# Stick-breaking attention: the scans of a pair of query rows queued behind the last low part of the pair ahead

## Chip, cores and metric

The kernel runs on one core of one Trainium2 chip. The metric is the device time of one execution in microseconds (us), as the median of the runs shown.

## The reference

A hybrid decoder layer over 1024 tokens of width 1024: a SwiGLU feed-forward block, a token mixer, a second feed-forward block, each on an RMS-normalised input, and a final normalisation. The mixer has 8 stick-breaking attention heads of width 64 and 4 gated recurrent heads (HGRN2) of width 128. The change lies in the attention heads:

```
z = einsum('bhqd,bhkd->bhqk', q_blk, k) * scale
causal = key_pos < q_pos
log_beta = log_sigmoid(z)
log_rest = where(causal, log_sigmoid(-z), 0)
tail = cumsum(log_rest, axis=3, reverse=True) - log_rest
w = where(causal, exp(log_beta + tail), 0)
o = einsum('bhqk,bhkd->bhqd', w, v)
```

So a weight is sigmoid(z) times the product of sigmoid(-z) over all later keys before the query. Everything is float32.

## The kernel before, in words

The tokens are stored in reverse order, so that "all keys between" is a running product from the left. Every float32 matmul is made of three in a rounded type: a number is split in a high part H (a rounding copy on ScalarE, L122) and a low part L (the source minus H, L123, on VectorE unless another engine is named). `split` does both.

The mixer works through four head pairs p; each pair p is two attention heads (a = 0, 1) and one recurrent head. `attend` (L761) runs the attention of a head pair: over two halves of the tokens (hf), two heads (a), and two pairs of query rows (qp) of two blocks of 128 rows each (j = 2 qp and 2 qp + 1). That makes 8 pairs of rows for each p and 32 in all.

For each block of rows, `stick` (L728) computes the scores of up to 512 keys at a time (TensorE, L743 to L746, in one of two banks ps_z), takes sigmoid(-z) into `rest` and sigmoid(z) into `beta` (ScalarE, L749 and L750), runs the running product over `rest` (VectorE's scan, L751; 128 to 512 columns) and multiplies it into `beta` (VectorE, L753; L755 multiplies the first column by the carry of the scan before). A block in the first half of the keys has two such steps chained by the carry, one in the second half has one, so a pair of rows has 4 or 2 scans, 96 in all.

When both blocks of a pair are done, the weights are transposed in units of two key blocks (m = qp to 3): TensorE transposes 3 or 4 blocks into one of two banks tp (L798, L799), ScalarE writes the high part wH, VectorE the low part wL (both L123's `split`, called in L804), each of two buffers, and TensorE multiplies them with the values into `po` (L769), one turn later than the transposes. A pair has 4, 3, 2 or 1 such units, 80 low parts in all. Here the first unit of a pair has 384 columns and the others 512. After two pairs, `po` is copied and added into the output `o_sb` (L811 on ScalarE, L813 on VectorE).

Between two calls of `stick` the generator yields, and the recurrent head takes a step of its own (`scan_half`, L840: small products on VectorE at L850, L869 and L895, predicated copies at L880, matmuls at L863 and L887). Behind each attention stretch come the projections of the next head pair (`project`, L663, three matmuls a step through L126 to L128; their outputs are read by L687, L697, L826, L836 and L837).

The order on each engine is not the order of the program. A scheduler lays all instructions out beforehand by its own timeline: on each engine it takes what it holds to be ready, earlier lines of the program first. A block `with tc.issue_after(ins):` adds an edge of order alone from each instruction inside that runs on the engine of `ins`: it is queued behind `ins` on that engine, without a semaphore. The kernel uses it already, among others for the products with the values (`in_turn`, L180, behind the last transpose).

Of the kernel before, what the change touches and what calls it, by code (L numbers as in the profile page):

```python
# [8 lines left out]
F32 = mybir.dt.float32  # L9
# [4 lines left out]
ALU = mybir.AluOpType  # L14
# [13 lines left out]
def hybrid_layer(ctx: ExitStack, tc, xT, gains, wg1, wu1, wd1, w_in, lbl, w_out, wg2, wu2, wd2, outT):  # L28
# [8 lines left out]
    nc = tc.nc  # L37
# [82 lines left out]

    def split(dH, dL, src, eng=None):
        nc.scalar.copy(dH, src)  # L122
        (eng or nc.vector).tensor_tensor(dL, src, dH.bitcast(F32), op=ALU.subtract)  # L123

    def mm3(ps, w, a, first, last):
        nc.tensor.matmul(ps, lhsT=w[0], rhs=a[0], start=first, stop=False)  # L126
# [3 lines left out]
    class Weights:  # L130
# [5 lines left out]
        def load(self, src, eng=None):  # L136
            r = self.raw.tile([P, self.width], F32, tag="raw", name="raw")
            nc.sync.dma_start(r, src)
            H = self.unit.tile([P, self.width], F32R, tag="uH", name="uH")
            L = self.unit.tile([P, self.width], F32R, tag="uL", name="uL")  # L140
            split(H, L, r, eng)
            return H, L
# [34 lines left out]
    def pe(ins):  # L177
        last_pe[:] = [ins.ins]

    def in_turn():  # L180

        return tc.issue_after(last_pe[0]) if last_pe else nullcontext()
# [54 lines left out]
    def norm_h(hf, g0, cols=slice(0, HALF), eng=None):  # L237
        for r in row_rstd(hf, cols):
            yield
        for c in range(NKC):  # L240
            if cols.start == 0:
                h[c, hf] = [hp.tile([P, HALF], F32R, tag=n, name=n) for n in ("hH", "hL")]
            t = xp.tile([P, HALF], F32, tag="x", name="hf")[:, cols]
            nc.vector.scalar_tensor_tensor(t, x[c, hf][:, cols], gn[:, g0 + c:g0 + c + 1], r,
                                           op0=ALU.mult, op1=ALU.mult)
            split(h[c, hf][0][:, cols], h[c, hf][1][:, cols], t, eng(c) if eng else None)
            yield
# [6 lines left out]
    def ffn(wg, wu, wd, order, prepare, on_x, on_half, pieces, g0, shared):  # L254
        one, two = order
        with ExitStack() as st:
# [22 lines left out]
            def entry(src, pool=None, eng=None):  # L279

                p, tH, tL = (hx, "bH", "bL") if pool is hx else (unit, "uH", "uL")
                H = p.tile([P, HALF], F32R, tag=tH, name=tH)
                L = p.tile([P, HALF], F32R, tag=tL, name=tL)
                split(H, L, src, eng)
                return H, L
# [368 lines left out]
    with ExitStack() as mix:  # L654
# [52 lines left out]
        def project_vi(p, vs, vg):  # L707

            ws = [W.load(w_in[VI + 4 * p + i], nc.gpsimd) for i in range(4)]
            for b2 in range(4):  # L710
# [14 lines left out]
                vg += [t[:, 0], t[:, 1]]  # L725
                yield

        def stick(q, k, a, j):  # L728

            out = {}  # L730
            S = q[j // 4][a]
            qc = slice((j % 4) * P, (j % 4 + 1) * P)
            carry = None
            for kh in range(j // 4, 2):
                b0 = max(j, 4 * kh)
                n = (4 * kh + 4 - b0) * P
                nw = max(n, 256)
                z0 = nw - n
                kc = slice(HALF - nw, HALF)
                H, L = k[kh][0][a], k[kh][1][a]  # L740
                z = ps_z.tile([P, HALF], F32, tag="z", name="z")
                diag = carry is None
                nc.tensor.matmul(z[:, :nw], lhsT=S[:, qc], rhs=H[:, kc], start=True, stop=False)  # L743
                pe(nc.tensor.matmul(z[:, :nw], lhsT=S[:, qc], rhs=L[:, kc], start=False, stop=not diag))
                if diag:
                    nc.tensor.matmul(z[:, z0:z0 + P], lhsT=ident_b, rhs=negm, start=False, stop=True)  # L746
                rest = mp.tile([P, HALF], F32, tag="rest", name="rest", bufs=3)
                beta = mp.tile([P, HALF], F32, tag="beta", name="beta", bufs=5)
                nc.scalar.activation(rest[:, :n], z[:, z0:nw], AF.Sigmoid, scale=-1.0)  # L749
                nc.scalar.activation(beta[:, :n], z[:, z0:nw], AF.Sigmoid)  # L750
                nc.vector.tensor_tensor_scan(rest[:, :n], rest[:, :n], rest[:, :n],  # L751
                                             1.0 if diag else carry, ALU.mult, ALU.bypass)
                nc.vector.tensor_tensor(beta[:, 1:n], beta[:, 1:n], rest[:, :n - 1], op=ALU.mult)  # L753
                if not diag:
                    nc.vector.tensor_tensor(beta[:, 0:1], beta[:, 0:1], carry, op=ALU.mult)  # L755
                carry = rest[:, n - 1:n]
                for b in range(b0, 4 * kh + 4):
                    out[b] = beta[:, (b - b0) * P:(b - b0 + 1) * P]
            return out

        def attend(p, q, k, vs, hfs=(0, 1)):  # L761

            later = []

            def products(po, vs, a, qp, m, H, L):
                for i in range(2):
                    b = 2 * m + i
                    for w in (H, L):
                        nc.tensor.matmul(po[:, (qp % 2) * 256:(qp % 2) * 256 + 256],  # L769
                                         lhsT=vs[b // 2][:, b % 2, a], rhs=w[:, 256 * i:256 * i + 256],  # L770
                                         start=m == qp and i == 0 and w is H,
                                         stop=m == 3 and i == 1 and w is L)

            def turn(*args):
                while later:
                    products(*later.pop())
                if args:
                    later.append(args)

            for hf in hfs:  # L780
                ot = xp.tile([P, HALF], F32, tag="x", name="o_sb")
                ov = ot.rearrange("p (q j t) -> p q j t", q=2, j=2)
                for a in range(2):
                    rows = slice(64 * a, 64 * a + 64)
                    po = ps_po.tile([P, HALF], F32, tag="po", name="po", bufs=1)
                    for qp in (2 * hf, 2 * hf + 1):
                        w0 = stick(q, k, a, 2 * qp)
                        yield
                        w1 = stick(q, k, a, 2 * qp + 1)
                        yield  # L790
                        for m in range(qp, 4):
                            tp = ps_tp.tile([P, HALF], F32, tag="tp", name="tp")
                            H = mp.tile([P, HALF], F32R, tag="wH", name="wH")
                            L = mp.tile([P, HALF], F32R, tag="wL", name="wL")
                            for i in range(2):
                                b = 2 * m + i
                                if b > 2 * qp:
                                    pe(nc.tensor.transpose(tp[:, 256 * i:256 * i + P], w1[b], ident))  # L798
                                pe(nc.tensor.transpose(tp[:, 256 * i + P:256 * i + 256], w0[b], ident))  # L799
                            lo = P if m == qp else 0  # L800
                            if m == qp:
                                nc.gpsimd.memset(H[:, :P].bitcast(F32), 0.0)
                                nc.gpsimd.memset(L[:, :P].bitcast(F32), 0.0)
                            split(H[:, lo:], L[:, lo:], tp[:, lo:])  # L804
                            with in_turn():
                                turn(po, vs, a, qp, m, H, L)
                    turn()
                    pv = po.rearrange("p (q j t) -> p q j t", q=2, j=2)
                    low = slice(64 - 64 * a, 128 - 64 * a)
                    for j in range(2):  # L810
                        nc.scalar.copy(ov[rows, :, j], pv[rows, :, 1 - j])  # L811
                    for j in range(2):
                        nc.vector.tensor_tensor(ov[rows, :, j], ov[rows, :, j], pv[low, :, 1 - j], op=ALU.add)  # L813
                o[2 * p, hf] = ot
# [217 lines left out]
        for n, _ in enumerate(attend(3, q, k, vs, (1, 0))):  # L1032
            next(scan)
            for _ in range({0: 1, 2: 1, 4: 1, 6: 1, 8: 1, 9: 1, 10: 1, 11: 1, 12: 1, 13: 1, 14: 1, 15: 1}.get(n, 0)):
                next(outs, None)
            if n == 8:
                state = out_half(3, 1, K[1], Q[1], *scans[1], vg, state)
            if n == 10:
                head_norms([(o[7, 1], True, 31, gate[1]), (o[6, 1], False, 27, None)])
            if n == 10 + 1:  # L1040
                mix_in(7, 1)
                mix_in(6, 1)
# [124 lines left out]
```

## Time and profile before

| what | value |
|---|---|
| median of 3 runs | 1984.62 us (1983.78 to 1987.51) |
| the profiled execution, its own time | 1987.7 us |
| its span | 1986.0 us |
| TensorE busy (matmul) | 1924.8 us, 97% |
| VectorE busy | 1343.5 us, 68% |
| ScalarE busy | 804.4 us, 41% |
| GpSimd busy | 948.0 us, 48% |
| scans, L751 | 96, 98.4 us in all |
| products, L753 | 96, 61.2 us in all |
| low parts of the weights, wL at L123 | 80, 49.4 us in all |

The span runs from the first to the last instruction of the profile. In the rows PE is TensorE, PEld its weight loads, DVE is VectorE, ACT is ScalarE, POOL is GpSimd. Busy time is the time in which an engine shows at least one instruction. Ends of matmuls are modelled and may overlap the next. A row of a timeline has the start from the span's beginning, the duration, engine, line, operation, what it writes and reads with shapes, and in brackets the idle time of its engine just before it and what ended it; rows in order of time may merge neighbours of one kind (x2).

### The profile page before, as it was taken

Reading aid. Unit: us, or ns where it says so; the run is one execution under the profiler, and the core shown is the slowest. Engines: PE = TensorE matmul, PEld = TensorE weight load, DVE = VectorE, ACT = ScalarE, POOL = GpSimd, SP = SyncE. Lnnn points to the kernel's source line nnn. Section 1 sums busy time; section 2 is a strip of 40 time slices with the busy share of each in tenths; the row PEclk is TensorE's granted clock in tenths of the full one; section 3 lists DMA queues with packets and bytes.
Section 4 is the critical chain, followed back from the end, with each engine's and each line's share of the span. In section 5 each row is a group of like instructions: output and inputs, shape, how many; then the busy total and the mean of one; then the engine's idle time right before and its main releaser. Section 6 shows DMA issues by size and latency. Waiting matters only on the chain.

```text
span 1986.0 us, 29345 instructions
## 1 busy us (share of the span) xinstructions
PE 1924.8 (97%) x10938; PEld 1589.0 (80%) x10938; DVE 1343.5 (68%) x1898; ACT 804.4 (41%) x1489; POOL 948.0 (48%) x815
## 2 busy tenths in 40 slices
PE   9899999999999999999999999999999999999997
PEld 7678888887888787887987977878778878888886
DVE  7966676667456736838648469669776666674476
ACT  6333323324444444535435445444333223344443
POOL 5245566557757432322233252001465565577585
PEclk9999999999999999999999999999999999999999
DMA  5134445346765421110111121211253454457544
GB/s 205 50 117 149 148 157 173 133 148 203 229 200 188 140 64 38 39 43 23 33 54 28 38 80 40 84 64 65 90 173 126 152 186 149 148 182 227 191 165 154
DMA packets 107823, 242.07 MB, mean 122 GB/s; under 512 B 10400, under 2 KB 12448, under 8 KB 107680
## 3 DMA queue, kind: packets, MB, share of 16 engines
q1 hardware_dynamic: 107392, 240.16, 36.7%
q8 instruction: 86, 1.41, 0.3%
q14 instruction: 57, 0.47, 0.1%
q10 hardware_dynamic: 288, 0.02, 0.0%
HBM read 169.89 MB, written 66.06 MB: 119 GB/s over the span
## 4 chain that ended last, share of the span: by engine, by line
PE 78%; DVE 9%; POOL 6%; issue 3%; DMA 2%; ACT 2%; SPq 0%; POOLq 0%; DVEq 0%; ACTq 0%
PE acc L126 17%; PE acc L128 17%; PE acc L127 17%; PE pj L126 3%; PE pj L128 3%; PE pj L127 3%; DMA raw<-in_wd_dram 2%; PE po L769 2%; PE pv L126 2%; PE pv L128 2%; PE pv L127 2%; PE wo L126 1%; DVE rest L751 1%; PE wo L127 1%; PE wo L128 1%
## 5 line engine op out<-in xcount | busy, mean ns | idle before, releaser
L122 ACT CAST uH<-raw 128x512 fp32r<-128x512 f32 x360 | 215.0, 619 | 499.8 <-POOL raw L354 187.9
L123 DVE TENSOR_TENSOR uL<-raw,uH 128x512 fp32r<-128x512 f32 x308 | 287.1, 949 | 167.9 <-ACT uH L122 167.7
L126 PE MATMUL acc<-hH,uH 128*128 128x512 f32 x704 | 280.4, 399 | 11.6 <-ACT uH L122 6.4
L127 PE MATMUL acc<-hL,uH 128*128 128x512 f32 x704 | 276.5, 393 | 0.3 <-DVE hL L228 0.2
L128 PE MATMUL acc<-hH,uL 128*128 128x512 f32 x704 | 271.1, 395 | 0.7 <-DVE uL L123 0.7
L123 DVE TENSOR_TENSOR bL<-raw,bH 128x512 fp32r<-128x512 f32 x140 | 168.7, 1211 | 136.0 <-ACT bH L122 117.8
L123 POOL TENSOR_TENSOR bL<-raw,bH 128x512 fp32r<-128x512 f32 x140 | 203.1, 1459 | 106.6 <-ACT bH L122 103.9
L122 ACT CAST bH<-raw 128x512 fp32r<-128x512 f32 x280 | 160.5, 618 | 188.5 <-PE acc L127 79.1
L373 DVE TENSOR_TENSOR c<-c,acc 128x512 f32<-128x512 f32 x280 | 186.9, 679 | 64.4 <-PE acc L128 62.1
L127 PE MATMUL acc<-bL,bH 128*128 128x512 f32 (+1 forms) x576 | 220.8, 383 | 0.9 <-DVE bL L123 0.9
L126 PE MATMUL acc<-bH 128*128 128x512 f32 (+1 forms) x576 | 221.2, 384 | 0.0
L128 PE MATMUL acc<-bH,bL 128*128 128x512 f32 (+1 forms) x576 | 219.1, 383 | 0.0
L126 PE MATMUL acc<-bH,uH 128*128 128x512 f32 x480 | 186.7, 389 | 0.6 <-ACT uH L122 0.6
L127 PE MATMUL acc<-bL,uH 128*128 128x512 f32 x480 | 186.7, 389 | 0.0
L128 PE MATMUL acc<-bH,uL 128*128 128x512 f32 x480 | 186.7, 389 | 0.0
L126 PEld LDWEIGHTS acc<-hH,uH 128*128 128x128 f32 x704 | 133.7, 190 | 51.9 <-ACT uH L122 19.0
L128 PEld LDWEIGHTS acc<-hH,uL 128*128 128x128 f32 x704 | 132.9, 189 | 35.3 <-DVE uL L123 8.3
L127 PEld LDWEIGHTS acc<-hL,uH 128*128 128x128 f32 x704 | 133.7, 190 | 28.1 <-DVE hL L228 1.5
L352 POOL TENSOR_TENSOR raw<-raw 128x512 f32<-128x512 f32 x40 | 60.0, 1501 | 194.7 <-DVE uL L123 194.7
L442 POOL TENSOR_TENSOR raw<-raw 128x512 f32<-128x512 f32 x20 | 27.0, 1352 | 263.8 <-DMA raw<-in_wd_dram 244.0
L123 POOL TENSOR_TENSOR uL<-raw,uH 128x512 fp32r<-128x512 f32 x52 | 70.1, 1354 | 155.6 <-ACT uH L122 152.3
L127 PEld LDWEIGHTS acc<-bL,bH 128*128 128x128 f32 x576 | 108.3, 188 | 22.2 <-DVE bL L123 1.3
(237 smaller groups left out, 4321.3 us busy)
## 6 DMA issues: line engine op xcount, KB each, us to landing
raw<-in_wd_dram SPq DMA_DIRECT2D x74, 512.0 KB, 4.3
a<-c SPq DMA_DIRECT2D x140, 256.0 KB, 3.2
raw<-a SPq DMA_DIRECT2D x70, 512.0 KB, 4.7
raw<-in_wg_dram SPq DMA_DIRECT2D x40, 512.0 KB, 4.8
raw<-in_wu_dram SPq DMA_DIRECT2D x40, 512.0 KB, 4.6
w<-raw SPq DMA_DIRECT2D x40, 512.0 KB, 2.8
raw<-w SPq DMA_DIRECT2D x40, 512.0 KB, 3.8
raw<-in_w_in_dram SPq DMA_DIRECT2D x56, 256.0 KB, 2.7
```

Source lines behind the costliest of these rows:

```text
L122: nc.scalar.copy(dH, src)
L123: (eng or nc.vector).tensor_tensor(dL, src, dH.bitcast(F32), op=ALU.subtract)
L126: nc.tensor.matmul(ps, lhsT=w[0], rhs=a[0], start=first, stop=False)
L127: nc.tensor.matmul(ps, lhsT=w[0], rhs=a[1], start=False, stop=False)
L128: pe(nc.tensor.matmul(ps, lhsT=w[1], rhs=a[0], start=False, stop=last))
L352: tt(a22, a21, a22, op=ALU.add)
L373: nc.vector.tensor_tensor(out, a, ps, op=ALU.add)
L442: tt(a22, a21, a22, op=ALU.add)
L751: nc.vector.tensor_tensor_scan(rest[:, :n], rest[:, :n], rest[:, :n], 1.0 if diag else carry, ALU.mult, ALU.bypass)
L769: nc.tensor.matmul(po[:, (qp % 2) * 256:(qp % 2) * 256 + 256], lhsT=vs[b // 2][:, b % 2, a], rhs=w[:, 256 * i:256 * i + 256], start=m == q ...
```

## The change

`split` returns its subtraction. A list holds the last low part of the pair of rows traced last (that of m = 3), and the scans of every later `stick` are queued behind it on VectorE. It carries over from one head, half and head pair to the next; only the two blocks of the very first pair have no such edge. Nothing else of the source changes.

```diff
     def split(dH, dL, src, eng=None):
         nc.scalar.copy(dH, src)
-        (eng or nc.vector).tensor_tensor(dL, src, dH.bitcast(F32), op=ALU.subtract)
+        return (eng or nc.vector).tensor_tensor(dL, src, dH.bitcast(F32), op=ALU.subtract)
...
+        last_low = []
+
         def stick(q, k, a, j):
...
-                nc.vector.tensor_tensor_scan(rest[:, :n], rest[:, :n], rest[:, :n],
-                                             1.0 if diag else carry, ALU.mult, ALU.bypass)
+                with tc.issue_after(last_low[0]) if last_low else nullcontext():
+                    nc.vector.tensor_tensor_scan(rest[:, :n], rest[:, :n], rest[:, :n],
+                                                 1.0 if diag else carry, ALU.mult, ALU.bypass)
...
-                            split(H[:, lo:], L[:, lo:], tp[:, lo:])
+                            low = split(H[:, lo:], L[:, lo:], tp[:, lo:])
                             with in_turn():
                                 turn(po, vs, a, qp, m, H, L)
+                        last_low[:] = [low.ins]
```

## Rows read from the trace of the kernel before

**Rows 1.** Stages: start:end, length, busy of PE, PEld, DVE, ACT, POOL, clock, DMA.

```profile
842.40:896.10 53.70, 53.70 (x369) 47.97 (x368) 19.07 (x40) 18.66 (x34) 11.59 (x11) 1.00 0.13 40
896.10:976.10 80.00, 75.85 (x830) 63.31 (x829) 67.19 (x124) 42.72 (x96) 26.14 (x47) 1.00 0.14 35
...
1171.60:1259.60 88.00, 81.11 (x802) 66.81 (x803) 77.36 (x141) 42.45 (x92) 23.50 (x41) 0.98 0.18 54
```

**Rows 2.** TensorE in order of time, a projection inside the second stretch.

```profile
906.29 0.39 PE L127 MATMUL pj<-hL,uH 128*128 128x512 f32 x1
906.52 0.40 PE L128 MATMUL pj<-hH,uL 128*128 128x512 f32 x1
```

**Rows 3.** VectorE in order of time, first and last border with early scans.

```profile
771.83 0.67 DVE L751 TENSOR_TENSOR_SCAN rest<-rest 128x256 f32<-128x256 f32 x1
...
776.37 0.68 DVE L123 TENSOR_TENSOR wL<-tp,wH 128x512 fp32r<-128x512 f32 x1
...
1242.44 1.28 DVE L751 TENSOR_TENSOR_SCAN rest<-rest 128x512 f32<-128x512 f32 x1
...
1245.64 1.49 DVE L123 TENSOR_TENSOR wL<-tp,wH 128x512 fp32r<-128x512 f32 x2 [0.27 <-ACT wH L122]
```

**Rows 4.** VectorE in order of time, scans between the second and third head pair.

```profile
972.74 1.22 DVE L751 TENSOR_TENSOR_SCAN rest<-rest 128x512 f32<-128x512 f32 x1
...
1004.15 1.28 DVE L751 TENSOR_TENSOR_SCAN rest<-rest 128x512 f32<-128x512 f32 x1 [3.89 <-ACT rest L749]
```

**Rows 5.** VectorE in order of time, border behind a first pair of rows.

```profile
904.93 0.68 DVE L123 TENSOR_TENSOR wL<-tp,wH 128x512 fp32r<-128x512 f32 x1
905.53 0.67 DVE L751 TENSOR_TENSOR_SCAN rest<-rest 128x256 f32<-128x256 f32 x1
...
906.65 1.77 DVE L751 TENSOR_TENSOR_SCAN rest<-rest 128x512 f32<-128x512 f32 x1
...
910.06 0.68 DVE L123 TENSOR_TENSOR wL<-tp,wH 128x512 fp32r<-128x512 f32 x1
...
911.87 1.28 DVE L751 TENSOR_TENSOR_SCAN rest<-rest 128x512 f32<-128x512 f32 x1 [0.40 <-ACT rest L749]
```

**Rows 6.** ScalarE in order of time, the rounding copy ahead of a late low part.

```profile
905.62 0.59 ACT L122 CAST wH<-tp 128x512 fp32r<-128x512 f32 x1
```

**Rows 7.** VectorE in order of time, a border already in the new order.

```profile
962.94 0.56 DVE L753 TENSOR_TENSOR beta<-beta,rest 128x383 f32<-128x383 f32 x1
963.99 0.23 DVE L880 COPY_PREDICATED near<-mask,sc_ps 128x64 f32<-128x64 uint8 x1 [0.49 <-PE sc_ps L863]
964.25 0.77 DVE L813 TENSOR_TENSOR o_sb<-o_sb,po 64x256 f32<-64x256 f32 x2
964.93 0.50 DVE L895 TENSOR_TENSOR Q<-Q,tots 128x256 f32<-128x256 f32 x1
965.47 1.16 DVE L123 TENSOR_TENSOR wL<-tp,wH 128x384 fp32r<-128x384 f32 x2
```

**Rows 8.** VectorE in order of time, a low part that waits for its rounding copy.

```profile
916.04 0.69 DVE L123 TENSOR_TENSOR wL<-tp,wH 128x512 fp32r<-128x512 f32 x1 [0.56 <-ACT wH L122]
```

**Rows 9.** Groups of VectorE, 896.1 to 976.1: count, busy, mean ns, idle before.

```profile
L751 DVE TENSOR_TENSOR_SCAN rest<-rest 128x512 f32<-128x512 f32 (+3 forms) x23 | 23.7, 1029 | 5.5 <-ACT rest L749 5.3
L753 DVE TENSOR_TENSOR beta<-beta,rest 128x511 f32<-128x511 f32 (+3 forms) x23 | 14.3, 628 | 1.0
L123 DVE TENSOR_TENSOR wL<-tp,wH 128x512 fp32r<-128x512 f32 (+1 forms) x20 | 12.3, 629 | 1.5 <-POOL wH L802 0.8 <-ACT wH L122 0.6
```

**Rows 10.** VectorE in order of time, waits of the second and last stretch.

```profile
953.32 0.75 DVE L813 TENSOR_TENSOR o_sb<-o_sb,po 64x256 f32<-64x256 f32 x2 [1.23 <-PE z L746]
...
1219.73 0.43 DVE L751 TENSOR_TENSOR_SCAN rest<-rest 128x128 f32<-128x128 f32 x1 [0.83 <-ACT rest L749]
```

**Rows 11.** Groups of TensorE, 680 to 1400: products with the low parts.

```profile
L769 PE MATMUL po<-wL,v 128*128 128x256 f32 x160 | 44.0, 297 | 12.8 <-DVE wL L123 12.7
```

## Prediction

> **What bounds the kernel now.** I read the windows by stage first, with the four attention stretches of the mixer and the projections between them as stages; then the rows of VectorE in order of time across the borders between pairs of query rows; last, who makes TensorE wait for a low part. All of the change lies in the attention stretches: 80 us for each of the first three head pairs and 88 us for the last, 328 us of the span. In the 80 us that begin at 896.1, VectorE is busy for 67.2 us and TensorE shows 75.9 us; in the 53.7 us of projections ahead of them TensorE is busy throughout and VectorE for 19.1 us [rows 1]. The stages alternate, so idle time of VectorE is free in a projection and may cost time in an attention stretch.
>
> TensorE's 75.9 us overstate it. Two matmuls of a projection in a row begin 0.23 us apart while each shows 0.40 us [rows 2]: the records overlap, and a TensorE that shows 0.40 us for a matmul every 0.5 us is half empty and still looks busy. VectorE's records hardly overlap, so its 67.2 us are work. By the busy shares as they stand TensorE would be the bound (95% against 84%) and a wait added on VectorE would cost nothing. The Trainium skill, "Perfetto Trace Analysis", section "Identifying the Most-Contended Engine", says that matmul busy time is no measure of how near TensorE is to its limit, and that for VectorE occupancy is a fair one; by that rule the added wait below counts in full, by the bare shares the sum would be zero. The sum does without the sentence: it follows from the starts in [rows 2].
>
> **What the change moves.** It adds no instruction and takes none away. Each scan gets an edge of issue order alone behind the last low part (the subtraction that writes wL) of the pair ahead; no semaphore is added, no DMA, and no queue but VectorE's is ordered by hand. Since the order of every engine comes from a scheduler, the others may be laid out anew too.
>
> How much is moved is read from VectorE's rows. In program order there are 32 pairs of rows, so 31 borders, with 96 scans and 80 low parts. Matching them in order of time, 44 scans at 28 borders start ahead of the last low part of the pair before them; the first is the scan at 771.83, whose pair ahead writes its last low part at 776.37, and the last is the one at 1242.44, ahead of the second of two low parts from 1245.64 [rows 3]. At three borders (the last one inside each of the first three stretches) the order is already that of the change. Three of the 28 lie between two head pairs: the scan at 972.74 is followed by VectorE's wait of 3.89 us before the scan at 1004.15, so moving it costs nothing [rows 4]. That is covered by the projections, and if they were shorter by some 25 us it would cost the scan's 1.2 us. 25 borders are left, 6 in each of the first three stretches and 7 in the last.
>
> **What one border costs.** At 904.93 a low part ends the half of a pair that was ready early. VectorE then scans twice, at 905.53 and 906.65, and the last low part of the pair comes at 910.06 [rows 5]. Under the change nothing of the next pair may fill that time. The last two low parts need transposes on TensorE, a rounding copy on ScalarE and then VectorE. The copy of such a part began at 905.62 and took 0.59 us [rows 6], so the low part could follow at about 906.2: VectorE is without the scan for 0.6 us, and then does the two low parts 3 us earlier than now. This is the kind of border behind the first pair of rows, where half of the low parts fill the wait; 8 of the 25 are such.
>
> Behind the other pairs, all or nearly all low parts wait for the last scan. The trace has one border of that kind already in the new order [rows 7]: the last product of the pair, at 962.94 for 0.56 us, ends at 963.50, and the low parts begin at 965.47. Bare, that is 1.97 us. Other work (a predicated copy, two additions of the output, a product of the recurrent heads) fills all but 0.49 us of it. So the bounds for 25 borders are:
> - below: nothing, where other work fills the wait;
> - above: 8 x 0.6 + 17 x 1.97 = 38.3 us, with no filler at all.
>
> I take 0.5 us a border, the 0.49 us of the row that is the thing itself. Another wait for a rounding copy with no scan let in, at 916.04, was 0.56 us [rows 8]. There is filler for it: of the 67.2 us in the stretch, scans take 23.7, products 14.3 and low parts 12.3 [rows 9], the small products by the carry another 1.0 at most, which leaves 15.9 us for eight pairs, 2.0 each, against the 1.5 us that the border of [rows 7] used. 25 x 0.5 = 12.5 us.
>
> Against it stand waits that later scans or earlier low parts swallow. VectorE waits 0.40 us for a sigmoid before the scan at 911.87 [rows 5], and it will come there later by about that much. It waits 1.23 us before the output's addition at 953.32, for products that come behind late low parts [rows 10]; I take half, 0.6. In the last stretch 0.83 us goes before the scan at 1219.73 [rows 10]. Together 3 x 1.0 + 0.83 = 3.8 us. Sum: 12.5 - 3.8 = +8.7 us.
>
> What stands behind VectorE in its queue while it waits: the scans of the next pair, then their products, and so TensorE's transposes of that pair. What comes earlier: TensorE's products with the values, and with them the two buffers of high and low parts. The last pair of each stretch has nothing behind it and no price.
>
> The profiled execution took 1987.7 us (span 1986.0, 1.7 around it), 3.1 us above the median of 1984.62. On it the sum makes 1996.4; on the median, which I predict, 1993.3.
>
> **Rivals.**
> *Faster: the low parts, no longer behind scans, keep TensorE fed.* In the mixer TensorE waits 12.7 us for low parts [rows 11], and each scan with its product puts about 2 us ahead of one. If all of it goes and VectorE's waits are filled, the time is 1984.6 - 12.7 = 1971.9; if half, 1978.3. The place is the order after 904.93; it decides from a wait per border under 3.8 / 25 = 0.15 us. For it: the filler of 2.0 us a pair. Against it: VectorE idles for 12.8 us in a stretch of 80, and there a work-conserving order is hard to better. The Trainium skill, "Perfetto Trace Analysis", section "Optimization Strategies", advises freeing the matmul engine from the engines that it waits for; on this rule alone the change gains.
>
> *No change: the waits are covered.* Filler takes the 0.5 us as well, or TensorE does projection work meanwhile that it would have done behind the stretch. 1984.6, give or take 4. For it: matmuls of the next projections do run inside the stretches, [rows 2] among them. Against it: what can be pulled forward is bounded by buffers that the running head pair holds. That the edge changes nothing is excluded by the 44 scans.
>
> *Slower by more: bare waits.* Without filler at the right moment, up to +38.3, 2022.9. It needs a chain of the recurrent heads that is never ready in time, which [rows 7] speak against.
>
> **Numbers.** A measurement of this kernel can tell about 0.2%, 4.0 us, from no change. Forecast of +8.7: 0.40; bare waits: 0.08; so slower 0.48. Covered: 0.28. TensorE fed: 0.24. The likeliest is 1993.3, and its own range, at 0.25 to 0.8 us a border, is 1987 to 2001. The range of 8 in 10 reaches down to 1975, most of the faster rival, and up to 2012, some 70% of the bare price.
>
> **What would show it.** Right: no scan ahead of the last low part of the pair before; low parts that wait for the rounding copy with more than the 0.6 us a stretch of now; fewer waits of VectorE for the sigmoid; stretches longer by 2 to 3 us each, and projections between them unchanged. TensorE's 12.7 us behind low parts should fall even so. Wrong: stretches of 80 us or less, or VectorE's idle time inside them unchanged; then filler or TensorE's order counted for more than I gave them. If the time grows between the stretches, the step that all of the change lies inside them has failed.

## The result and the profile after

The changed kernel takes 2015.44 us (median of 4 runs) against 1984.20 for the kernel before: 31.2 us slower, a ratio of 1.0158 with a 95% interval of 1.0138 to 1.0179. The forecast was +8.7 us with a range up to 2012. The direction was right, the size was 3.6 times too small, and the time lies outside the range.

The stages of the changed kernel, in the columns of [rows 1] (a stretch runs from the third scan of a head pair, the second in the last, to the end of its last low part): start and end, length, busy time of TensorE, its weight loads, VectorE, ScalarE, GpSimd, granted clock, DMA.

```profile
759.20:847.20 88.00, 80.39 (x828) 66.41 (x827) 66.59 (x122) 42.63 (x96) 27.78 (x47) 0.94 0.12 31
847.20:901.10 53.90, 53.90 (x371) 48.18 (x370) 20.71 (x41) 18.79 (x34) 11.59 (x11) 1.00 0.14 40
901.10:988.00 86.90, 79.27 (x828) 65.70 (x827) 66.50 (x122) 42.72 (x96) 27.54 (x47) 0.96 0.12 32
...
1042.00:1130.70 88.70, 81.20 (x833) 67.07 (x832) 66.64 (x122) 42.55 (x96) 27.52 (x47) 0.94 0.12 31
...
1192.20:1288.10 95.90, 88.49 (x812) 71.62 (x812) 76.98 (x142) 42.14 (x92) 23.36 (x41) 0.95 0.16 50
```

The four attention stretches take 359.5 us in place of 328.0 (three of 80.0 and one of 88.0): +31.5, or 31.5 / 25 = 1.26 us a border, not the 0.5 taken. The stages between them have their old lengths, and no scan stands ahead of the last low part of the pair before it any more (44 did). VectorE's idle time in the stretches, length less busy time, grows from 49.1 us to 82.8, +33.7. This alone doesn't make VectorE's waits the cause: an engine whose work stays the same must idle longer in a longer stretch, and ScalarE's idle time grows by 32 us too. (The profiled span grew by 26.4 only: the work ahead of the first stretch and behind the last, which the change does not touch, took 5.3 us less in this execution.)

Where the wait sits is seen at the border of [rows 5]. VectorE in order of time, changed kernel:

```profile
909.94 0.68 DVE L123 TENSOR_TENSOR wL<-tp,wH 128x512 fp32r<-128x512 f32 x1
911.12 0.30 DVE L885 COPY_PREDICATED near<-mask,sc_ps 128x64 f32<-128x64 uint8 x1 [0.49 <-PE sc_ps L868]
...
912.17 0.68 DVE L123 TENSOR_TENSOR wL<-tp,wH 128x512 fp32r<-128x512 f32 x1
914.30 0.69 DVE L123 TENSOR_TENSOR wL<-tp,wH 128x512 fp32r<-128x512 f32 x1 [1.45 <-ACT wH L122]
```

The third low part comes early, as foretold. Before the fourth, for which the scans wait, VectorE idles for 1.45 us: it needs its rounding copy on ScalarE. What that copy waited for, ScalarE in order of time:

```profile
913.68 0.59 ACT L122 CAST wH<-tp 128x512 fp32r<-128x512 f32 x1 [2.45 <-PE tp L803]
```

And what TensorE did in those 2.45 us, in order of time:

```profile
910.27 0.27 PE L803 MATMUL tp<-ident,beta 128*128 128x128 f32 x1
...
910.97 0.50 PE L126 MATMUL pj<-hH,uH 128*128 128x512 f32 x1
...
912.46 0.39 PE L126 MATMUL pj<-hH,uH 128*128 128x512 f32 x1
...
913.04 0.27 PE L802 MATMUL tp<-ident,beta 128*128 128x128 f32 x1
```

Between the transposes of the third and of the fourth unit stand seven matmuls of the next head pair's projections, 910.97 to 912.7. They stood there before too: the two of [rows 2] are of the same seven. Then VectorE scanned meanwhile. Now it waits.

The other border of this kind in the same stretch has longer waits and no projection matmul in the way. VectorE in order of time, changed kernel:

```profile
939.75 0.42 DVE L900 TENSOR_TENSOR Q<-Q,tots 128x256 f32<-128x256 f32 x1 [1.88 <-PE sc_ps L892]
...
942.09 0.69 DVE L123 TENSOR_TENSOR wL<-tp,wH 128x512 fp32r<-128x512 f32 x1 [1.31 <-ACT wH L122]
```

TensorE in order of time, ahead of it:

```profile
937.42 0.36 PE L773 MATMUL po<-wL,v 128*128 128x256 f32 x1 [1.65 <-DVE wL L123]
...
938.07 0.42 PE L803 MATMUL tp<-ident,beta 128*128 128x128 f32 x1
938.29 0.42 PE L802 MATMUL tp<-ident,beta 128*128 128x128 f32 x1
...
939.06 0.64 PE L892 MATMUL sc_ps<-Q,K 128*32 128x32 f32 x16
...
940.44 0.41 PE L802 MATMUL tp<-ident,beta 128*128 128x128 f32 x1
```

Here TensorE itself waited 1.65 us for the first low part of the pair. Then the transposes of the third unit, a matmul group of the recurrent head (sc_ps) and those of the fourth follow, at the lower clock told of at the end. VectorE's wait of 1.88 us is for that sc_ps: an operation of the recurrent head stands ahead of the third low part in its queue. So the wait has more than one source.

At a fourth pair's border projection matmuls stand ahead again. VectorE in order of time, changed kernel:

```profile
963.83 0.60 DVE L757 TENSOR_TENSOR beta<-beta,rest 128x255 f32<-128x255 f32 x2
967.18 0.22 DVE L885 COPY_PREDICATED near<-mask,sc_ps 128x64 f32<-128x64 uint8 x1 [2.74 <-PE sc_ps L868]
...
968.25 0.56 DVE L123 TENSOR_TENSOR wL<-tp,wH 128x384 fp32r<-128x384 f32 x1
```

TensorE in order of time, ahead of the same low part:

```profile
961.74 0.40 PE L127 MATMUL pj<-hL,uH 128*128 128x512 f32 x1
...
965.64 0.39 PE L126 MATMUL pj<-hH,uH 128*128 128x512 f32 x1
...
967.04 0.33 PE L803 MATMUL tp<-ident,beta 128*128 128x128 f32 x1
```

The pair's last product ends at 964.4. Projection matmuls run on until 966.0, the first transpose shown begins at 967.04, and VectorE's wait of 2.74 us is again for a product of the recurrent head (sc_ps). Over the whole second stretch such products hold VectorE up the longest of what has grown. Its waits there, for whom, us in total, times, longest:

```profile
DVE near L885 <- PE sc_ps L868: 3.5, 3, 2.7
DVE wL L123 <- ACT wH L122: 3.5, 3, 1.4
DVE Q L900 <- PE sc_ps L892: 3.3, 2, 1.9
```

And before, beside the 0.6 for ACT wH L122 in [rows 9]:

```profile
DVE Q L895 <- PE sc_ps L887: 1.2, 1, 1.2
DVE near L880 <- PE sc_ps L863: 0.5, 1, 0.5
```

The waits for sc_ps grew from 1.7 to 6.8 us, those for rounding copies from 0.6 to 3.5. In the last stretch, where TensorE's other work is the output projection, the filler on VectorE waits itself. Waits of VectorE there: for whom, us in total, times, longest:

```profile
DVE wL L123 <- ACT wH L122: 8.6, 7, 2.7
DVE x L973 <- PE wo L128: 7.5, 4, 3.0
```

The additions of the output projection (x, L968 before and L973 now) waited 2.5 us in that stretch before. One of them waits 2.96 us at 1237.92, ahead of the low part at 1239.44 in VectorE's queue.

One thing came as the faster rival has it. Group of TensorE's products with the low parts, which answers to [rows 11]:

```profile
L773 PE MATMUL po<-wL,v 128*128 128x256 f32 x160 | 47.2, 315 | 7.6 <-DVE wL L123 7.4
```

TensorE's wait for low parts fell from 12.7 to 7.4 us. It was no gain: all of TensorE's idle time in the stretches (length less busy time) grew from 19.4 to 30.2 us.

### The profile page after: what moved, and what is told of

Read it like the earlier page. It is cut to its first block, busy times and chain, and to the rows that moved or that the text cites. A ratio compares the mean times of both kernels' runs of the same rounds, so it can differ in the third digit from the quotient of the medians.

```text
span 2012.4 us, 29317 instructions
## 1 busy us (share of the span) xinstructions
PE 1941.8 (96%) x10938; PEld 1601.4 (80%) x10938; DVE 1342.8 (67%) x1898; ACT 804.2 (40%) x1489; POOL 951.9 (47%) x815
## 4 chain that ended last, share of the span: by engine, by line
PE 80%; DVE 9%; POOL 4%; issue 3%; ACT 2%; DMA 2%; POOLq 0%; SPq 0%; ACTq 0%; DVEq 0%
PE acc L126 18%; PE acc L128 18%; PE acc L127 18%; PE pj L126 3%; PE pj L127 3%; PE pj L128 3%; PE po L773 2%; DVE rest L755 2%; PE pv L126 2%; PE pv L128 2%; PE pv L127 2%; PE wo L126 1%; PE wo L127 1%; PE wo L128 1%; DMA raw<-in_wd_dram 1%
## 5 line engine op out<-in xcount | busy, mean ns | idle before, releaser
L122 ACT CAST uH<-raw 128x512 fp32r<-128x512 f32 x360 | 214.8, 618 | 496.6 <-POOL raw L354 186.8
L122 ACT CAST bH<-raw 128x512 fp32r<-128x512 f32 x280 | 160.6, 618 | 188.5 <-PE acc L127 78.6
L442 POOL TENSOR_TENSOR raw<-raw 128x512 f32<-128x512 f32 x20 | 26.6, 1331 | 263.6 <-DMA raw<-in_wd_dram 263.6
```

Source lines behind the costliest of these rows:

```text
L442: tt(a22, a21, a22, op=ALU.add)
```

## Experiments

### Which borders cost

The list of the last low part was kept behind some pairs of rows only, and emptied behind the others:

```diff
-                        last_low[:] = [low.ins]
+                        last_low[:] = [low.ins] if qp == 0 else []
```

with `qp == 1` in the second kernel and `qp > 1` in the third. That is 8, 7 and 10 of the 25 borders; the expectations count 8, 8 and 9.

> Edges only behind the first pair of rows of a head (8 of the 25 borders). Theory 'each border has its own wait': the costs of the parts add up to the whole 31 us; VectorE's waits in the changed kernel at the two such borders of a stretch (0.49 + 1.45 and 1.88 + 1.31 us) say about 2.5 us a border, less what was waited before, so +10 to +18 us. Theory 'the clock': a border alone does not starve TensorE long enough for its granted clock to fall, so this part costs under 5 us and the three parts together under 15.

2000.52 us, ratio 1.0073 (1.0048 to 1.0098): +15.2, in the middle of the first theory's range and over the 5 us of the second. (The clock fell here too, to between 0.96 and 0.98 in the stretches.)

> Edges only behind the second pair of rows (8 borders). Each border has its own wait: the changed kernel waits 1.21 and 0.73 us at the two of a stretch, so +5 to +9 us. The clock: under 5 us, granted clock as before.

1984.27 us, ratio 0.9996 (0.9986 to 1.0006): no change, where 5 to 9 us were expected. VectorE does wait behind the second pairs of this kernel. In order of time, second stretch:

```profile
913.73 1.41 DVE L687 SCALAR_TENSOR_TENSOR q<-pj,q 64x512 fp32r<-64x512 f32 x2 [1.37 <-ACT q L685]
```

At the second such border of the stretch it waits 1.40 us for a product of the recurrent head. So a wait of VectorE at a border is not a cost by itself.

> Edges only behind the third and fourth pairs of rows (9 borders inside the stretches, and the three between head pairs). Each border has its own wait: the changed kernel waits 2.74 us behind the fourth pair and little behind the third, so +8 to +14 us. The clock: under 5 us.

1991.10 us, ratio 1.0029 (1.0018 to 1.0040): +5.7, just over the 5 us of the second theory and under the first one's range. First and last stretch of this kernel:

```profile
758.90:839.10 80.20, 76.01 (x829) 63.35 (x829) 64.27 (x122) 42.82 (x97) 25.61 (x47) 1.00 0.13 34
1170.50:1265.10 94.60, 86.88 (x802) 70.84 (x803) 77.05 (x142) 42.77 (x93) 22.99 (x41) 0.95 0.16 51
```

The loss lies mostly in the last stretch, 94.6 us against 88.0. In the first VectorE idles for 15.9 us instead of 12.8, and the stretch is 0.2 us longer.

The three add up to 19.8 us of the 31.2. So the borders behind the first pairs, which the prediction priced lowest (at most 0.6 us each), cost most, 15.2 / 8 = 1.9 us each, and about a third of the loss appears only when all borders are queued (roughly: the interval of the first kernel alone is 10 us wide). The first theory is right for the first pairs, and neither is right for the sum. In the first of these kernels the wait is the one seen above; VectorE in order of time:

```profile
913.24 0.69 DVE L123 TENSOR_TENSOR wL<-tp,wH 128x512 fp32r<-128x512 f32 x1 [1.43 <-ACT wH L122]
```

### One scan set free

```diff
-                with tc.issue_after(last_low[0]) if last_low else nullcontext():
+                with tc.issue_after(last_low[0]) if last_low and (j % 2 or not diag) else nullcontext():
```

> All edges but that of the first scan of each pair of rows, which may go ahead of the last low part as before; 16 or so second scans stay queued. If one scan of 1.2 us is enough to bridge the wait, the time is that of the kernel before within 5 us; if the bridge needs both scans, it keeps half or more of the 31 us.

1985.94 us, ratio 1.0003 (0.9993 to 1.0014). One scan per pair ahead of the last low part takes back the whole loss, though all other scans stay queued. The bridge over the wait is one scan and its product: 1.1 us where the scan has 256 columns, as behind the first pairs (0.67 us and 0.42), and 1.9 us with 512.

### What the low parts wait for

The projection matmuls that fill TensorE in a stretch (48 groups of three) were queued by hand, six groups behind the last transpose of each pair of rows. The same was put into both kernels:

```diff
         def project(units, steps=None, at=()):
...
-                    with in_turn() if steps else nullcontext():
+                    mark = None if steps else next(fill[0], None)
+                    with tc.issue_after(mark) if mark else in_turn() if steps else nullcontext():
...
+                        marks.append(last_pe[0])
...
+            fill[0] = iter([i for i in marks for _ in range(6)])
+            marks.clear()
             gate = project_silu(GG + 2 * p, "FF")
...
+            fill[0] = iter(())
```

> The kernel before, with the matmuls of the next head pair's projections that fill TensorE inside an attention stretch (gate, queries, keys: 48 groups of three) spread by hand: six groups behind the last transpose of each pair of rows. If VectorE sets these stretches, TensorE's order matters little: within 6 us of the kernel before. If TensorE's order sets them, it moves by more, either way.

> The changed kernel with the same spread, so that no such projection matmul can stand ahead of the transposes of its pair of rows. Theory 'the low parts are late because their transposes stand in TensorE's queue behind projection matmuls': its distance to the run above falls from 31 to under 15 us. Theory 'they are late because of the two buffers of high and low parts': it stays over 25.

The kernel before becomes 2009.68 us, ratio 1.0127 (1.0111 to 1.0143), the changed one 2015.28, ratio 1.0157 (1.0142 to 1.0172). So the first expectation failed, +24 us and not within 6. Where that went shows in the stages. The first three stretches of the kernel before with the spread, in the columns of [rows 1]:

```profile
756.30:837.20 80.90, 75.68 (x781) 60.66 (x781) 65.46 (x118) 39.72 (x90) 24.68 (x45) 0.96 0.08 23
897.90:981.10 83.20, 77.86 (x782) 62.38 (x781) 65.31 (x119) 39.59 (x88) 24.19 (x45) 0.94 0.08 20
1041.80:1121.40 79.60, 74.22 (x758) 59.56 (x757) 65.75 (x119) 38.92 (x87) 23.65 (x45) 0.94 0.08 22
```

And of the changed kernel with it:

```profile
754.90:836.80 81.90, 74.74 (x784) 59.89 (x785) 65.26 (x119) 40.94 (x92) 26.26 (x45) 0.98 0.08 23
896.90:978.50 81.60, 75.94 (x785) 60.41 (x785) 65.46 (x120) 40.72 (x91) 25.84 (x45) 0.96 0.08 21
1038.60:1123.10 84.50, 78.08 (x780) 62.38 (x779) 65.14 (x119) 39.26 (x88) 26.07 (x45) 0.92 0.08 20
```

The stretches of the kernel before take 243.7 us against 240.0, though 50 to 70 of 830 matmuls have left each; the stages between (837.2 to 897.9, 60.7 us, against 53.7) hold them now. In time the second expectation held. With the projections behind the transposes, the edges lengthen the first three stretches by 248.0 - 243.7 = 4.3 us, where they cost 263.6 - 240.0 = 23.6 us with the scheduler's own order of TensorE. In time the two differ by 5.6 us, where the plain kernels differ by 31.2.

But the low parts don't come sooner. VectorE's wait for them in the second stretch of the changed kernel with the spread:

```profile
DVE wL L123 <- ACT wH L122: 9.5, 6, 4.0
```

The waits for rounding copies are 9.5 us (4.0 of them behind the last pair, which has nothing queued behind it) against 3.5 without the spread; those for the recurrent heads' products fell from 6.8 to 2.4 (1.1 and 1.3). By this, projection matmuls held up the recurrent heads' products, but they are not the only reason why low parts are late. The changed kernel's time has not moved (2015.28 us against 2015.44): the difference shrank because the kernel without edges became slower.

A looser spread left twelve groups free and the last behind the sixth pair:

```diff
-            fill[0] = iter([i for i in marks for _ in range(6)])
+            fill[0] = iter([None] * 12 + [i for i in marks[:6] for _ in range(6)])
```

> The kernel before, with the projection matmuls spread again, but two pairs of rows earlier: twelve groups are free and the last group stands behind the sixth pair, so that all of them still fit in the stretch. Within 8 us of the kernel before; the stretches between keep their 53.7 us, where the first spread made them 60.7.

> The changed kernel with this spread. Theory 'transposes behind projection matmuls': some matmuls may again stand ahead of the transposes, but six groups (4.2 us) a pair at most, so part of the 31 us comes back: 5 to 20 us faster than the changed kernel. If the two spread kernels differ by 25 us or more, the queue of TensorE is not the reason.

2004.76 us, ratio 1.0089 (1.0068 to 1.0109), for the kernel before: +20.2, so it too loses more than expected, and the stages between take 57.2 us, not 53.7. 2015.13, ratio 1.0135 (1.0110 to 1.0159), for the changed one: none of the 31 us came back as time, where 5 to 20 were expected. The distance of the two is 10.4 us, under the 25 that would have cleared TensorE's queue. Both spreads make the price of the edges small and the kernel without edges slow. They show that the price depends on TensorE's order; that projection matmuls ahead of the transposes make up the loss, they don't show, and they are no remedy.

### Buffers

The Trainium skill, "Perfetto Trace Analysis", section "Optimization Strategy", says that the same gap repeating on the engine that should be full can mean too few buffers. The high and low parts of the weights got a third buffer each in the changed kernel:

```diff
-                            H = mp.tile([P, HALF], F32R, tag="wH", name="wH")
-                            L = mp.tile([P, HALF], F32R, tag="wL", name="wL")
+                            H = mp.tile([P, HALF], F32R, tag="wH", name="wH", bufs=3)
+                            L = mp.tile([P, HALF], F32R, tag="wL", name="wL", bufs=3)
```

> The changed kernel with three buffers for the high and the low parts of the weights in place of two. Theory 'buffers': at least 10 us of the 31 come back. Theory 'TensorE's queue': within 6 us of the changed kernel.

2014.23 us, ratio 1.0145 (1.0130 to 1.0160): 1.2 us from the changed kernel. The gaps repeat, but not for want of these buffers. The two banks for the transposes were not tried, so it stays open what a third would give.

### The price of VectorE's time

One more subtraction, result unused, was queued on VectorE behind the last product of each pair of rows, in either kernel:

```diff
+        last_mul = []
...
-                nc.vector.tensor_tensor(beta[:, 1:n], beta[:, 1:n], rest[:, :n - 1], op=ALU.mult)
+                last_mul[:] = [nc.vector.tensor_tensor(beta[:, 1:n], beta[:, 1:n], rest[:, :n - 1], op=ALU.mult).ins]
...
+                        spare = mp.tile([P, HALF], F32, tag="spare", name="spare", bufs=1)
+                        with tc.issue_after(last_mul[0]):
+                            nc.vector.tensor_tensor(spare, q[0][0].bitcast(F32), q[0][0].bitcast(F32), op=ALU.subtract)
                         for m in range(qp, 4):
```

> The kernel before with one more subtraction of 512 columns on VectorE (0.68 to 0.95 us, result unused) behind the last product of each pair of rows, 32 in all, 22 to 30 us. If VectorE's time in the stretches counts in full, as the prediction's sum has it: +18 us or more. If TensorE sets the stretches: under 8.

1996.01 us, ratio 1.0056 (1.0035 to 1.0077): +11.4. Stretches of this kernel:

```profile
757.40:841.90 84.50, 79.49 (x828) 65.96 (x827) 72.86 (x133) 42.46 (x96) 26.58 (x47) 0.96 0.12 32
895.70:978.80 83.10, 78.08 (x829) 64.85 (x829) 72.92 (x133) 42.38 (x96) 26.59 (x47) 0.98 0.13 33
1032.60:1114.50 81.90, 76.75 (x819) 63.73 (x819) 71.90 (x132) 41.48 (x94) 26.56 (x47) 0.98 0.12 32
1177.70:1270.10 92.40, 84.04 (x801) 68.44 (x800) 81.47 (x150) 42.77 (x92) 27.10 (x43) 0.94 0.16 52
```

VectorE is busy for 299.2 us of them, 20.2 more than before, and they are 13.9 us longer: 69% of the added work counts. (The granted clock is lower there too, 0.94 to 0.98, and may have its part in it.) Both readings that I set against each other failed: added time of VectorE is neither free, as TensorE's busy share would have it, nor counted in full.

> The changed kernel with the same 32 subtractions. If VectorE waits there for low parts, as the theory has it, the subtractions lie in that wait: at most half of what they cost in the run above, and the time stays within 12 us of the changed kernel. If the loss comes from elsewhere, they cost the same as in the run above.

2036.58 us, ratio 1.0244 (1.0210 to 1.0277): 21.1 us slower than the changed kernel, so the expectation failed. The subtraction did not lie in the wait; the wait grew. VectorE in order of time, this kernel:

```profile
921.54 0.69 DVE L123 TENSOR_TENSOR wL<-tp,wH 128x512 fp32r<-128x512 f32 x1 [0.17 <-ACT wH L122]
928.00 0.69 DVE L123 TENSOR_TENSOR wL<-tp,wH 128x512 fp32r<-128x512 f32 x1 [5.77 <-ACT wH L122]
```

TensorE in order of time in that wait:

```profile
921.86 0.63 PE L126 MATMUL pj<-hH,uH 128*128 128x512 f32 x1
922.28 0.63 PE L127 MATMUL pj<-hL,uH 128*128 128x512 f32 x1
...
926.17 0.39 PE L126 MATMUL pj<-hH,uH 128*128 128x512 f32 x1
...
926.75 0.27 PE L807 MATMUL tp<-ident,beta 128*128 128x128 f32 x1
```

The scheduler laid sixteen projection matmuls (920.79 to 926.17) ahead of the last transposes, where seven stood. At this border that is the changed kernel's own wait, enlarged: VectorE waits here for as long as TensorE has other work ahead of the transposes.

### The clock

The granted clock of TensorE fell inside the stretches, from 1.00 (0.98 in the last) to between 0.94 and 0.96. Four more matmuls ahead of each pair's first transposes were to keep TensorE busy in its waits:

```diff
+                            if m == qp:
+                                for _ in range(4):
+                                    nc.tensor.matmul(tp, lhsT=k[0][0][a][:, :P], rhs=k[0][0][a], start=True, stop=True)
```

> The changed kernel with four more matmuls of 512 columns ahead of the first transposes of each pair of rows (128 in all, 0.23 us each, 29 us of TensorE, results overwritten). Theory 'part of the loss is the granted clock': TensorE's clock inside the stretches goes from 0.94-0.96 back to 0.98 or more, and the time stays within 8 us of the changed kernel or falls. If the clock costs nothing, TensorE's added work shows: 10 to 29 us slower than the changed kernel.

2038.46 us, ratio 1.0272 (1.0255 to 1.0290): 23.0 us slower than the changed kernel. The clock of the four stretches was 0.98, 0.91, 0.96 and 0.98, so it did not come back throughout, and the run doesn't tell what the clock costs. Most of the added time is not in the stretches (363.8 us against 359.5) but in the stages between, which hold more matmuls and take 186.5 us against 169.4.

## Why the prediction was right in direction and wrong in size

**What bounds the stretches.** Half right. The loss lies inside the stretches, and time taken from VectorE does cost; but work added to it counted only to 69%, waits at the second pairs cost nothing, and moving TensorE's matmuls about cost 20 to 24 us. Neither engine alone sets the stretch. On this the Trainium skill's rule ("Perfetto Trace Analysis", "Identifying the Most-Contended Engine") was nearer than the bare busy shares, by which the change would have been free.

**What the change moves.** Right: 44 scans, the three between head pairs at no price, stages between unchanged.

**The price of a border.** This is the step that failed, "I take 0.5 us a border". It measured 1.26 us on average and 1.9 us behind the first pairs, where at most 0.6 had been allowed. The error was in the sentence on those: the copy began at 905.62, "so the low part could follow at about 906.2". That is the third of four low parts. The edge waits for the fourth, whose transposes stood in TensorE's queue behind seven projection matmuls, and VectorE's fourth low part came at 910.06 in [rows 5]. The trace of before had that queue, [rows 2] are a piece of it, and I priced the chain as if each engine did its step as soon as it could. At the other first pair of each of the first three stretches no projection matmul is in the way, and VectorE waits even longer, 1.88 and 1.31 us: TensorE stood still for a low part first, then ran at the lower clock. The border of [rows 7], taken as the pattern, was one where the transposes began at 963.84, right behind the product that ends at 963.50. Filler did not help as reckoned either: it came from chains that wait for TensorE themselves (6.8 us for the recurrent heads in the second stretch, 7.5 us for the output projection in the last), and an operation that waits blocks the low part behind it. How the 31 us divide among these sources no run shows.

**The waits that vanish.** Right. The waits of 0.40, 1.23 and 0.83 us at the three places are gone from the changed kernel, and TensorE's wait for low parts fell by 5.3 us. The rest outweighed them.

**The rivals.** Faster and no change are refuted by the interval. The bare waits, given 0.08, were the nearest: 2022.9 against 2015.44. Their mechanism, a chain of the recurrent heads that is not ready in time, is seen: in the second stretch it holds the larger part of VectorE's new waits (5.1 us more, against 2.9 more for rounding copies). It hangs on TensorE's queue in its turn, as the spread suggests. The upper end of the range, 70% of this price, was too low.

**What stays open.** About a third of the loss (11.4 us) comes only with all edges together. TensorE's granted clock is a candidate: length times the share not granted is 18.9 us in the four stretches, against 1.8 before, so 17.1 us of TensorE's full speed were lost. This is no price: a stretch of 79.6 us with a clock of 0.94 stands among those of the first spread, no longer than before, if with 758 matmuls in place of 830. No run separates it from the scheduler's new layout of the other engines.

## What to carry to other kernels

To price an edge of issue order, look at what its target waits for at the end of its chain, in the queue of each engine on the chain: count what stands ahead of the last step there, and not only the latency of the steps. Where a scheduler lets other work run ahead, that work can be the bridge over waits that the trace of before does not show as waits. Leaving one operation free to bridge (here one scan with its product, 1.1 to 1.9 us) kept the whole time. And idle time of one engine is not yet a price: the edges behind the second pairs made VectorE wait and cost nothing.

## What the hardware showed

TensorE's clock fell after idle time inside a stretch whose busy share is 91%. Windows of 4 us of TensorE in the changed kernel: length, busy time, clock, DMA.

```profile
932.00:936.00 4.00, 2.27 (x44) 1.00 0.05 15
936.00:940.00 4.00, 2.58 (x25) 0.73 0.22 66
940.00:944.00 4.00, 3.38 (x32) 0.85 0.00 0
```

After 1.7 us without a matmul in one window and 1.4 in the next, half of the time between 936 and 940 was at the lower of the two levels, 1.2 GHz: transposes began 0.21 us apart there (938.07 to 938.29 above), and 0.11 apart at the higher level, 2.4 GHz (932.51 to 932.62). The kernel before kept 1.00 in its second stretch and 0.98 in the last, [rows 1]. In the kernel with the added subtraction the projection matmuls ahead of a low part began 0.42 us apart (921.86 and 922.28 above) against the 0.23 of [rows 2], so there the lower clock lengthened the wait of VectorE.
